# First layer's mixing with tokens on partitions: split weights everywhere, and the 31-tap convolution as a 128-point Fourier transform

## The chip, the cores and the metric

The kernel runs on one core of a Trainium2 chip. The metric is device time in microseconds (us) of the whole program, median of the timed runs. One further execution was profiled; all rows below are from that one. Engine names are those of the profile: PE is TensorE, PEld its weight load, DVE is VectorE, ACT is ScalarE, POOL is GpSimd, SP is SyncE, whose queue issues nearly all transfers.

## The reference, cut to what matters

A decoder trunk of two layers, 256 tokens, width 1024, all in float32. Each layer is a half-step SwiGLU network, a mixing part and a second half-step network. The mixing part of the first layer, the one that is changed, is this:

```python
hn = rms_norm(h, mix_norm_g[0])
u = hn @ a_w_in[0]                                  # 1024 x (768 + 768 + 256)
a, gate, q_mem = u[..., :768], u[..., 768:1536], u[..., 1536:]
c = a * sigmoid(gate)
c = depthwise_causal_conv(c, taps=31) + dw_bias     # 768 channels
primary = silu(layer_norm(c, ln_g, ln_b))
mem_out = memory_attention(q_mem, rms_norm(mem), w_mem_kv[0], ...)   # 4 heads of 64, 256 memory rows
h = h + concatenate([primary, mem_out]) @ w_o[0]    # 1024 x 1024
```

The second layer's mixing part has attention over a shared key and value set in place of the convolution; its keys and values from the memory (`w_mem_kv[1]`) do not depend on the tokens, and the kernel makes them during the first layer's mixing part.

## The kernel before, in words

Weights stream from main memory in chunks of 128 x 2048 floats (1 MB) through three buffers `raw`. A chunk is used in one of two ways.

- Split: each half of 1024 columns is turned by ACT into `wh`, the part that one pass of PE takes (type fp32r), and by DVE into the rest, `wl = raw - wh` (`half_hi`, `half_chunk`, lines 199 to 226). There are four buffers of each. A product is then three one-pass terms: `wh` by the high part of the input, `wh` by its low part, `wl` by the high part (`mm3`, `mm3_tok`). In the networks the first two terms are one instruction of 512 columns (`mm2`).
- Whole: `raw` goes to PE as float32 (`raw_chunk`). PE then runs two instructions for each product.

The program is a chain of stages with PE working through nearly all of it: network `a` (names `ag`, `au`, `ao`), the first mixing part, network `b`, the shared keys and values (`kv`), network `c`, the second mixing part, network `d`.

The first mixing part (lines 801 to 1044) works with channels on partitions. `glu_in` makes the six 128-channel blocks of value (`ca`) and gate (`cg`), 256 token columns at a time; blocks 0 and 1 from split weights, blocks 2 to 5 from whole ones, and so is the query product `mq`. `conv` then adds the 31 taps of blocks 0 to 4 one tap at a time: `DVE_TAPS` of them as a multiply-add on DVE (line 892), `POOL_TAPS` as a product on ACT (line 883) and an addition on POOL (line 884). Block 5 goes to PE as 32 products with diagonal matrices `diag`, which ACT builds during the down projection of network `a` (line 798). The layer norm sums over channels with two sets of products (`lnm`, `lnv`). Meanwhile PE makes the memory keys and values of the next layer from whole weights (`mkv`), runs the attention of two pairs of heads (`am00`, `am01`) and opens the output projection (`oao`) with the attention's 256 rows, again from whole weights. The 768 rows of the convolution follow from split weights. The order around these steps is partly written by hand with `go`, partly left to the scheduler.

The second mixing part is built from named steps whose order on PE, DVE, ACT and POOL is one written list, `MIX1`; all its weights are split. The engines take their steps strictly in this order.

Of the kernel before, what the change touches and what calls it, by code (L numbers as in the profile page):

```python
# [32 lines left out]
PAD = TAPS - 1  # L33
# [10 lines left out]
SPLIT_CHUNKS = 2  # L44

DVE_TAPS = (14, 31, 0, 31, 18)
POOL_TAPS = (17, 0, 31, 0, 13)

HALF_CH = P // 2
SHIFTS = (TAPS + 1) // 2  # L50
PADH = PAD // 2
MEM_AT = 9
FIRST_CAT = 3

# [21 lines left out]
Q_AT = 6  # L76
CNR_AT = 4

# [15 lines left out]
V_TAP = 72  # L94
V_CB = V_TAP + CC * TAPS
V_LG = V_CB + CC
V_LB = V_LG + CC
V_PP = V_LB + CC
V_PB = V_PP + 4 * SHIFTS

V_QG = V_PB + 2
NV = V_QG + 2

G_MQ, G_MK, G_K, G_Q = 0, 1, 3, 4
NG = 5
# [4 lines left out]

@with_exitstack
def tile_kernel(ctx: ExitStack, tc: tile.TileContext, w, xT, memT, pos, vec, hg, const, out):
# [25 lines left out]
    nc.scalar.dma_start(vt[:, :V_TAP], vec[:, :V_TAP])  # L138
# [8 lines left out]
    onel = cp.tile([P, 1], F32, name="onel")  # L147
    nc.vector.memset(onel, 1.0 / PW)
    onem = cp.tile([P, P], F32, name="onem")
    nc.vector.memset(onem, 1.0 / PW)  # L150
# [18 lines left out]

    def tables(func):  # L170

        behind(nc.scalar.activation(warm, onec, func), state["func"])
# [20 lines left out]

    def raw_chunk():
        assert state["half"] == 0
        state["chunk"] += 1
        return load_chunk(state["chunk"] - 1)
# [84 lines left out]
    def y_both(name):  # L282
        whole = yp.tile([P, KD, 2, SEQ], F32, name=name + "w", tag="y")
        return y_tiles(name), whole[:, :, 0]

    def scaled_split(y, src, k, g, on_dve=False):

        if isinstance(y, tuple):
            y, yw = y
            if on_dve:  # L290
                nc.vector.tensor_scalar(yw[:, k], src, vt[:, g + k:g + k + 1], None, op0=ALU.mult)
                nc.scalar.activation(y[:, k, 0], src, AF.Copy, scale=vt[:, g + k:g + k + 1])
            else:
                nc.scalar.activation(yw[:, k], src, AF.Copy, scale=vt[:, g + k:g + k + 1])
                nc.scalar.activation(y[:, k, 0], yw[:, k], AF.Copy)
            nc.vector.tensor_tensor(y[:, k, 1], yw[:, k], y[:, k, 0].bitcast(F32), op=ALU.subtract)
            return
# [50 lines left out]
    def ffn(name, y, acc, nexts, store=False, both=False, hook=None, after=None, hook_down=None, r=None, plan=None):  # L348
# [98 lines left out]
        ys = [(y_both if both else y_tiles)(f"{name}y{i}") for i in range(len(nexts))]  # L447
        acc = new_acc(name + "acc")
        it = tiles_of(KD * KF // 8)
        for m in range(KD):  # L450
# [21 lines left out]
            last = both and m == KD - 1  # L472
            if last:
                square_sum(f"{name}q{m}", acc, x[:, m], False, nc.vector)
            for yy, g in zip(ys, nexts):
                state["ends"] = scaled_split(yy, x[:, m], m, g, last)
            if not last:
                square_sum(f"{name}q{m}", acc, x[:, m], m == 0)
# [35 lines left out]
    def proj(name, y, *uses):  # L514
# [3 lines left out]
        if isinstance(y, tuple):  # L518
            raw = raw_chunk()
            for k in range(KD):  # L520
                for t in range(NT):
                    mmul(os_[t][:, :n], y[1][:, k, t * P:(t + 1) * P], raw[:, k * n:(k + 1) * n],
                         start=k == 0, stop=k == KD - 1)
        else:
            per = HC // n
            for k0 in range(0, KD, per):
                wh, wl = half_chunk()
                for t in range(NT):
                    for i in range(per):
                        k = k0 + i  # L530
                        mm3_tok(os_[t][:, :n], wh, wl, y, t, k, slice(i * n, (i + 1) * n), k == 0, k == KD - 1)
# [35 lines left out]
    def queries(name, e, g, dst, pair0, defer):  # L567


        def use(t, o):  # L570
            ms = heads_norm(f"{name}s{t}", o, 4)
            qg = tp.tile([P, MW], F32, name=f"{name}t{t}", tag="tok")
            q3 = qg.rearrange("p (h d) -> p h d", d=HD)
            nc.vector.tensor_tensor(q3, o.rearrange("p (h d) -> p h d", d=HD), gain_b(g, 4), op=ALU.mult)
            v = tp.tile([P, 4], F32, name=f"{name}v{t}", tag="hv")
            nc.vector.tensor_scalar(v, ms, e[:, t:t + 1], None, op0=ALU.add)
            c = tp.tile([P, 4], F32, name=f"{name}c{t}", tag="hr")
            nc.gpsimd.tensor_tensor(c, v, mhalf[:, :4], op=ALU.pow)
            nc.vector.tensor_tensor(q3, q3, c[:, :, None].to_broadcast([P, 4, HD]), op=ALU.mult)
            def turn():  # L580
                to_heads_T(f"{name}p{t}", qg, dst, pair0, t, "sc")
            defer.append(turn)
        return use

    def attend_pair(name, qT, kT, v, vcol0, pair, causal, tag, done, o_tag=("mm", 4)):

        hs = [slice(e * HD, (e + 1) * HD) for e in range(2)]
        S = [psum(f"{name}s{e}", *(("mm", 4) if tag == "mm" else ("sc", 2))) for e in range(2)]
        spans = ((0, P), (P, 3 * P)) if causal else ((0, SEQ), (SEQ, 2 * SEQ))
        width = spans[1][1]  # L590
        opened = []
        for t, (lo, hi) in enumerate(spans):
            for e in range(2):

                i = mmul(S[e][:, lo:hi], qT[hs[e], pair, t * P:(t + 1) * P], kT[hs[e], pair, :hi - lo],
                         start=t == 0 or not causal, stop=not causal, skip_group_check=causal)
                if t:
                    behind(i, opened[e])
                opened.append(i)
        if causal:  # L600
            for e in range(2):

                mmul(S[e].rearrange("p (a b) -> p a b", b=2 * P)[:, :, :P], identb,
                     maskb[:, None, :].to_broadcast([P, 2, P]), start=False, stop=True, skip_group_check=True)
        yield

        nb = [tp.tile([P, NT], F32, name=f"{name}n{e}", tag="nb", bufs=4) for e in range(2)]
        for e in range(2):
            if causal:
                for t, (lo, hi) in enumerate(spans):  # L610
                    in_order("V", nc.vector.tensor_reduce(nb[e][:, t:t + 1], S[e][:, lo:hi], axis=AX.X, op=ALU.min))
            else:
                in_order("V", nc.vector.tensor_reduce(nb[e], S[e].rearrange("p (t k) -> p t k", t=NT), axis=AX.X,
# [57 lines left out]
    def go(head, n):  # L671
        for _ in range(n):
            next(head)
# [830 lines left out]
```

## Time and profile before

| | us |
|---|---|
| median of three timed runs (979.95 to 980.14) | 980.0 |
| span of the profiled execution, first to last instruction | 978.8 |
| PE busy | 971.9 |
| PEld busy | 848.1 |
| DVE busy | 727.8 |
| ACT busy | 592.4 |
| POOL busy | 132.4 |

Busy time of PE counts each matmul from its start to its modelled end, and successive matmuls overlap in it; what a matmul costs in a stream is the distance from one start to the next. The median lies 1.2 us above the span; that part lies outside the first and the last instruction. The granted clock of PE is 1.000 on average.

### The profile page before, as it was taken

To read this page: it belongs to the slowest core of one execution; us is meant where nothing else is said; L and a number is where in the kernel's file an instruction comes from. 1 tells how busy PE (TensorE), PEld (TensorE's weight loads), DVE (VectorE), ACT (ScalarE), POOL (GpSimd) and SP (SyncE) were. 2 spreads that over 40 slices of the span, in tenths; PEclk is the share of its full clock that TensorE was granted. 3 is DMA by queue.
4 is the path that set the end of the run, shared out by engine and by line. 5 is a ranking of instruction groups with operands and counts; after the bars stand their busy time and mean duration, and the time that the engine had idled before them with its cause. 6 is when DMAs were issued, how large, how long until landed. Compare 5 with 4: busy or idle time off the path is not lost.

```text
span 978.8 us, 15511 instructions
## 1 busy us (share of the span) xinstructions
PE 971.9 (99%) x5793; PEld 848.1 (87%) x5793; DVE 727.8 (74%) x1305; ACT 592.4 (61%) x1150; POOL 132.4 (14%) x154
## 2 busy tenths in 40 slices
PE   9999999999999999999999999999999999999998
PEld 6888888898779888888888888888897898888887
DVE  7888776679967777777766877776669578777663
ACT  6675577747667655555556655565547666555542
POOL 0121000128812000000122100000133130000000
PEclk9999999999999999999999999999999999999999
DMA  8655555533325555555555555455552255555550
GB/s 324 246 180 177 209 173 181 207 130 130 106 110 175 213 177 199 184 175 202 183 178 176 206 178 204 179 191 197 175 172 85 92 174 209 178 209 173 191 217 22
DMA packets 26427, 173.44 MB, mean 177 GB/s; under 512 B 3184, under 2 KB 4848, under 8 KB 6000
## 3 DMA queue, kind: packets, MB, share of 16 engines
q1 hardware_dynamic: 26064, 172.28, 50.9%
q8 instruction: 45, 0.74, 0.3%
q14 instruction: 30, 0.25, 0.1%
q10 hardware_dynamic: 288, 0.17, 0.1%
HBM read 171.39 MB, written 1.05 MB: 176 GB/s over the span
## 4 chain that ended last, share of the span: by engine, by line
PE 92%; DVE 4%; POOL 2%; ACT 1%; issue 1%; POOLq 0%
PE cg L175 7%; PE bg L175 6%; PE bu L175 6%; PE do L175 6%; PE co L175 6%; PE bo L175 6%; PE ao L175 6%; PE ag L175 6%; PE au L175 6%; PE dg L175 6%; PE cu L175 6%; PE du L175 6%; PE kv L175 3%; PE oao L175 2%; PE obo L175 2%; PE mkv L175 2%
## 5 line engine op out<-in xcount | busy, mean ns | idle before, releaser
L211 ACT ACTIVATE wh<-raw 128x1024 fp32r<-128x1024 f32 (+1 forms) x310 | 325.0, 1050 | 312.1 <-PE bg L175 27.5
L215 DVE TENSOR_TENSOR wl<-raw,wh 128x1024 fp32r<-128x1024 f32 (+1 forms) x310 | 376.9, 1218 | 178.6 <-ACT wh L211 177.7
L175 PE MATMUL ag<-y,wh 128*128 128x512 f32 x176 | 63.7, 397 | 0.0
L175 PE MATMUL bg<-oay,wh 128*128 128x512 f32 x176 | 63.5, 399 | 0.0
L175 PE MATMUL bu<-oay,wh 128*128 128x512 f32 x176 | 63.4, 398 | 0.0
L175 PE MATMUL au<-y,wh 128*128 128x512 f32 x176 | 63.1, 394 | 0.0
L175 PE MATMUL dg<-oby,wh 128*128 128x512 f32 x176 | 62.5, 392 | 0.0
L175 PE MATMUL cg<-by,wh 128*128 128x512 f32 x176 | 62.3, 392 | 0.0
L175 PE MATMUL du<-oby,wh 128*128 128x512 f32 x176 | 62.3, 391 | 0.0
L175 PE MATMUL cu<-by,wh 128*128 128x512 f32 x176 | 62.2, 392 | 0.0
L175 PE MATMUL co<-chs,wh 128*128 128x512 f32 (+1 forms) x198 | 61.9, 369 | 0.0
L175 PE MATMUL do<-dhs,wh 128*128 128x512 f32 (+1 forms) x198 | 61.9, 369 | 0.0
L175 PE MATMUL bo<-bhs,wh 128*128 128x512 f32 (+1 forms) x198 | 61.9, 369 | 0.0
L175 PE MATMUL ao<-ahs,wh 128*128 128x512 f32 (+1 forms) x198 | 61.9, 368 | 0.0
L175 PE MATMUL co<-chs,wl 128*128 128x256 f32 x176 | 49.7, 283 | 0.0
L175 PE MATMUL do<-dhs,wl 128*128 128x256 f32 x176 | 49.7, 283 | 0.0
L175 PE MATMUL bo<-bhs,wl 128*128 128x256 f32 x176 | 49.6, 283 | 0.0
L175 PE MATMUL ao<-ahs,wl 128*128 128x256 f32 x176 | 49.6, 283 | 0.0
L175 PE MATMUL bg<-oay,wl 128*128 128x256 f32 x176 | 49.5, 281 | 0.0
L175 PE MATMUL cg<-by,wl 128*128 128x256 f32 x176 | 49.5, 281 | 0.0
L175 PE MATMUL bu<-oay,wl 128*128 128x256 f32 x176 | 49.4, 281 | 0.0
L175 PE MATMUL dg<-oby,wl 128*128 128x256 f32 x176 | 49.4, 280 | 0.0
(947 smaller groups left out, 2430.0 us busy)
## 6 DMA issues: line engine op xcount, KB each, us to landing
raw<-in_w SPq DMA_DIRECT2D x158, 1024.0 KB, 4.8
raw<-in_w SPq DMA_DIRECT2D x5, 512.0 KB, 8.8
mT<-in_memT SPq DMA_DIRECT2D x1, 1024.0 KB, 7.4
out<-x SPq DMA_DIRECT2D x8, 128.0 KB, 1.7
raw<-in_w SPq DMA_DIRECT2D x2, 256.0 KB, 4.2
x<-in_xT SPq DMA_DIRECT2D x1, 512.0 KB, 7.3
x<-in_xT SPq DMA_DIRECT2D x2, 128.0 KB, 3.1
x<-in_xT SPq DMA_DIRECT2D x1, 256.0 KB, 5.3
```

What stands on the lines that cost most here:

```text
L175: return in_order("P", nc.tensor.matmul(*a, **k))
L211: state["act"] = nc.scalar.activation(wh[:, s], raw[:, s], AF.Copy)
L215: state["dve"] = nc.vector.tensor_tensor(wl[:, s], raw[:, s], wh[:, s].bitcast(F32), op=ALU.subtract)
```

## The change

All of the first mixing part is rewritten with tokens on partitions, as named steps in one written order, `MIX0`, like that of the second. The second part's functions `heads_pair`, `room_of` and `stepper` are now shared by both; its own order does not change.

- Every weight of the stage is split: value and gate, query, memory keys and values of the next layer, all eight row blocks of the output projection. That is 26 halves of 1024 columns where the stage had 10.
- Value and gate come in three groups (A, B, C) of 256 channels: inputs are the stationary operand, and 512 weight columns (256 value, 256 gate) stream.
- The convolution of a group is: three blocks of 128 rows (tokens 0 to 127, tokens 128 to 255, and a third one put together from the first 32 tokens of both halves, the last 32 of the first half and 32 rows of zeros), a forward transform by one 128 x 128 matrix (`F`), a product with the taps' spectrum (`z`, `y`), an inverse transform (`I`). Transforms are whole float32 products. The first 32 outputs of each half are taken from the third block (`e1`).
- The spectrum `spec` is made once during network `a` from a small table (`spectra`).
- The layer norm uses the statistics instructions of DVE (`b`, `L.a`), then the result is transposed back to channels on partitions (`L.T`).
- The query's gain moves into the memory key's (`gq`, index 2).

Four constants are loaded next to the memory input, and the conv taps leave the vector table. The memory input's scaled copy for the next layer (`next_mem`) is now made, split, in the down projection of network `a`, where the diagonals were built.

```diff
-        if isinstance(y, tuple):
-            raw = raw_chunk()
-            for k in range(KD):
-                for t in range(NT):
-                    mmul(os_[t][:, :n], y[1][:, k, t * P:(t + 1) * P], raw[:, k * n:(k + 1) * n], ...)
...
-def conv(c):
...
-            for i in range(nd + 1, nd + np_):
-                nc.scalar.activation(q, win(c, i), AF.Copy, scale=tap[c][i])
-                state["pool"] = nc.gpsimd.tensor_tensor(cv[:, c], cv[:, c], q, op=ALU.add)
...
-            for i in range(1, nd):
-                nc.vector.scalar_tensor_tensor(cv[:, c] if end else o, win(c, i), tap[c][i], o, ...)
...
+            nc.sync.dma_start(spec[:, S_F:S_G + P], wave[:, :2 * P])
+            nc.sync.dma_start(roots, wave[:3 * REACH, 2 * P:])
+            nc.sync.dma_start(tapw, taps)
+            nc.sync.dma_start(spec[:, S_BIAS:S_BIAS + PW], bias)
...
+    def spectra():
+        nc.scalar.activation(rootr, roots, AF.Copy)
+        nc.scalar.activation(tapr, tapw, AF.Copy)
+        nc.vector.tensor_tensor(tapr[low], tapw[low], tapr[low].bitcast(F32), op=ALU.subtract)
+        for i in range(3):
+            for at in range(512 * i, 512 * (i + 1), MW):
+                mmul(o[:, at % 512:at % 512 + MW], rootr[:, ...], tapr[:, c:c + MW], start=True, stop=True)
+            nc.scalar.activation(spec[:, 512 * i:512 * (i + 1)], o, AF.Copy)
...
+    def project(name, yy, first, ks, n):
+        per = HC // n
+        for k in ks:
+            wh, wl = halves[first + k // per][:2]
+            for t in range(NT):
+                mm3_tok(pss[name][t][:, :n], wh, wl, yy, t, k, slice(k % per * n, (k % per + 1) * n), ...)
...
+    def gated_group(name, g, first):
...
+            @step(f"{name}.s{t}")
+                state["func"] = A(nc.scalar.activation(sg[t], pss[name][t][:, MW:], AF.Sigmoid, scale=rc[:, t:t + 1]))
+            @step(f"{name}.h{t}")
+                V(nc.vector.scalar_tensor_tensor(h3[:, t, gs], pss[name][t][:, :MW], rc[:, t:t + 1], sg[t], ...))
+            @step(f"{name}.k{i}")
+                V(nc.vector.tensor_copy(h3[to * REACH:(to + 1) * REACH, 2, gs], h3[fr * REACH:(fr + 1) * REACH, t, gs]))
...
+            @step(f"{name}.F{b}")
+                mmul(out_of("X", b, n), spec[:, S_F:S_F + P], h3[:, bs, gs], start=True, stop=True)
+            @step(f"{name}.z{b}")
+                V(nc.vector.tensor_tensor(z1[:, bs], X, wide(S_A, whole, n), op=ALU.mult))
+                V(nc.vector.tensor_tensor(z2[high, bs], X[low], wide(S_B, low, n), op=ALU.mult))
+                V(nc.vector.tensor_tensor(z2[low, bs], X[high], wide(S_B, high, n), op=ALU.mult))
+            @step(f"{name}.y{b}")
+                G(nc.gpsimd.tensor_tensor(z1[:, bs], z1[:, bs], z2[:, bs], op=ALU.add))
+            @step(f"{name}.I{b}")
+                mmul(out_of("O", b, n), spec[:, S_G:S_G + P], z1[:, bs], start=True, stop=True)
+        @step(f"{name}.e02")
+            V(nc.vector.tensor_tensor(cv[:, :, gs], out_of("O", "02", 2), wide(S_BIAS, whole, 2), op=ALU.add))
+        @step(f"{name}.e1")
+            for t, fr in ((0, 2), (1, 0)):
+                V(nc.vector.tensor_tensor(cv[:REACH, t, gs], pss[name + "O1"][r, :MW], spec[r, S_BIAS + ...], op=ALU.add))
+            @step(f"{name}.b{t}")
+                V(nc.vector.bn_stats(bn[:, t, g], cv[:, t, gs]))
...
+    @step("L.a")
+            V(nc.vector.bn_aggr(agg[:, t], bn[:, t].rearrange("p g s -> p (g s)")))
+        V(nc.vector.tensor_scalar(var, agg[:, :, 1], EPS, None, op0=ALU.add))
+    @step("L.r")
+        G(nc.gpsimd.tensor_tensor(rl, var, mhalf[:, :NT], op=ALU.pow))
+    @step(f"L.z{t}")
+            V(nc.vector.tensor_scalar(cv[:, t], cv[:, t], agg[:, t, 0:1], rl[:, t:t + 1], ...))
+    @step(f"L.T{i}")
+            for c in range(2 * i, 2 * i + 2):
+                for t in range(NT):
+                    transp(pss["L", i][:, ...], cv[:, t, c * P:(c + 1) * P], ident)
...
+MIX0 = """
+hi0 hi1 lo0 hi2 A.0 zero lo1 hi3 lo2 hi4 A.1 lo3 lo4 A.2 hi5 lo5 A.3a hi6 B.0 lo6 cn hi7 A.3b cv ce cr lo7 B.1 hi8
...
+B.F1 hi12 A.F02 B.z1 C.0 A.z02 B.y1 A.F1 hi13 lo12 Q.1 A.y02 A.z1 lo13 A.y1 A.I02 q.s hi14 C.1 q.r A.e02 q.p lo14
...
+B.I02 C.h1 M.0 n0.mn1 n0.ex0 C.k1 C.k0 C.k2 B.e02 n0.ex1 n0.nm0 C.F02 B.e1 hi17 n0.tr0 n0.nm1 M.1 n0.ev0 C.z02 hi18
+n1.S lo17 hi19 C.y02 C.F1 n1.mn1 n0.tr1 M.2 C.z1 n1.ex1 n1.mn0 C.y1 n0.ev1 n1.ex0 n1.nm1 C.I02 B.b0 C.I1 xs C.e02
+M.3 C.e1 hi20 n1.nm0 C.b1 B.b1 n0.o hi21 C.b0 L.a n1.tr1 n0.hi lo18 n1.tr0 L.r K.t1 n1.ev0 n1.ev1 K.t0 L.z0 K.s1
+n1.o K.s0 L.z1 K.v1 n0.lo n1.hi L.T0 lo19 K.v0 L.T1 c0.s L.T2 o.6 c0.h n1.lo c1.s lo20 c1.h c2.s c0.l c2.h lo21 c3.s
...
```

Steps with `02` work on the first two blocks together, 512 columns; those with `1` on the third, 256. `L.z` takes 768 columns, `L.T0` to `L.T2` are twelve transposes. In `MIX0`, `hi` and `lo` are the two splits of a half, `Q` the query product, `M` and `K` the next layer's memory keys and values, `n0` and `n1` the two pairs of heads (`S` scores, `mn` minimum, `ex` exponential, `nm` division, `tr` transposes, `ev` their eviction, `o` the product with the values), `c` the norm's gain, silu and split per channel block, `o.k` the output rows of block k.

## Rows read from the trace of the kernel before

**Rows 1.** The head of the page: span, then busy time, share of the span and number of instructions of each engine.
```profile
span 978.8 us, 15511 instructions
PE 971.9 (99%) x5793; PEld 848.1 (87%) x5793; DVE 727.8 (74%) x1305; ACT 592.4 (61%) x1150; POOL 132.4 (14%) x154
```
**Rows 2.** Busy time by stretch: start and end, length, then PE, PEld, DVE, ACT, POOL busy (with instruction counts), granted clock, DMA share, GB/s. The stretches are all that lies before the first mixing part, the first mixing part, the second mixing part.
```profile
0.00:205.70 205.70, 204.22 (x1163) 176.16 (x1164) 156.66 (x281) 142.44 (x300) 19.80 (x23) 1.00 0.61 211
205.50:312.20 106.70, 105.29 (x633) 90.15 (x632) 87.46 (x199) 71.06 (x156) 51.98 (x70) 1.00 0.36 123
717.70:790.80 73.10, 72.61 (x599) 63.85 (x598) 54.47 (x141) 49.51 (x130) 25.10 (x26) 1.00 0.31 105
```
**Rows 3.** The chain that ended last, in order of time, in the first mixing part: start, length, engine, tile, line, count.
```profile
212.08 2.87 PE ca L175 x24
...
217.82 3.46 PE ca L175 x16
...
235.92 3.14 DVE cvp L892 x8
...
254.97 1.42 POOL hc L884 x2
...
267.73 1.19 PE am00s L175 x6
...
270.00 1.91 PE mkv L175 x4
271.91 2.59 PE lnm L175 x12
274.50 3.43 PE mkv L175 x8
277.94 0.87 PE am00pp L178 x8
...
280.53 2.68 PE lnv L175 x24
283.21 1.01 PE am00o L175 x8
...
297.01 0.22 PE mk1p L178 x2
...
312.18 0.35 PE bu L175 x2
```
**Rows 4.** Groups of PE instructions in the first mixing part: line, engine, operation, output and inputs, shape, count, then busy time, mean ns of one, idle time before them.
```profile
L175 PE MATMUL mkv<-raw,hc 128*128 128x512 f32 x32 | 14.5, 596 | 0.0
L175 PE MATMUL ca<-ay0w,raw 128*128 128x256 f32 x64 | 14.5, 379 | 0.0
L175 PE MATMUL cg<-ay0w,raw 128*128 128x256 f32 x64 | 14.5, 379 | 0.0
...
L175 PE MATMUL oao<-hc,raw 128*128 128x256 f32 x32 | 7.3, 382 | 0.5 <-ACT hc L668 0.5
L175 PE MATMUL cvp<-hc,diag 128*128 128x128 f32 x64 | 7.3, 275 | 0.0
L175 PE MATMUL mq<-raw,ay0w 128*128 128x256 f32 x32 | 7.1, 379 | 0.0
...
L175 PE MATMUL ca<-ay,wh 128*128 128x256 f32 x32 | 5.9, 285 | 0.0
...
L175 PE MATMUL am00s<-mk,q0T 64*128 64x256 f32 x8 | 1.4, 402 | 0.9 <-ACT q0T L511 0.9
```
**Rows 5.** The chain again, during network `a`: the memory keys and values of the first layer, split weights, 512 columns streaming.
```profile
60.18 10.92 PE mkv L175 x48
```
**Rows 6.** Groups of instructions of DVE and POOL over the whole span, shapes kept apart, columns as in rows 4.
```profile
L215 DVE TENSOR_TENSOR wl<-raw,wh 128x1024 fp32r<-128x1024 f32 x302 | 371.7, 1232 | 177.0 <-ACT wh L211 176.1
L892 DVE SCALAR_TENSOR_TENSOR cvp<-hc,vt,cvp 128x256 f32<-128x256 f32 x88 | 40.6, 484 | 1.5
...
L303 DVE SCALAR_TENSOR_TENSOR cy<-x,vt,cy 128x256 fp32r<-128x256 f32 x8 | 6.7, 843 | 0.6 <-ACT cy L302 0.6
L215 DVE TENSOR_TENSOR wl<-raw,wh 128x512 fp32r<-128x512 f32 x8 | 5.2, 688 | 1.6 <-ACT wh L211 1.6
...
L1240 DVE TENSOR_SCALAR room<-room 128x256 f32<-128x256 f32 x14 | 4.7, 364 | 0.1
...
L303 DVE SCALAR_TENSOR_TENSOR y<-x,vt,y 128x256 fp32r<-128x256 f32 x8 | 3.5, 480 | 0.0
...
L884 POOL TENSOR_TENSOR hc<-hc,cq 128x256 f32<-128x256 f32 x58 | 42.5, 735 | 12.6 <-ACT cq L883 8.8 <-POOL hc L884 0.2
```
**Rows 7.** PE in order of time in the second mixing part: scores, transposes and value products of masked pairs of heads.
```profile
756.99 0.93 PE L175 MATMUL a4s<-kvs,q1T 64*128 64x128 f32 x8
...
758.18 0.88 PE L178 MATMUL a2pp<-cst,room 128*128 128x128 f32 x6
759.00 0.87 PE L175 MATMUL a1o<-room,kvs 128*64 128x256 f32 x8
759.80 0.93 PE L175 MATMUL a5s<-kvs,q1T 64*128 64x128 f32 x8
```
**Rows 8.** The chain in the second mixing part where it runs through DVE: one split.
```profile
741.58 1.13 DVE wl L215
```
**Rows 9.** Busy time by stretch, as in rows 2, at the time when the four constants would land.
```profile
30.00:38.00 8.00, 8.00 (x49) 7.00 (x48) 7.93 (x17) 6.30 (x14) 0.00 (x0) 1.00 0.59 217
```

More of the change, by code (lines that the diff above doesn't have):

```diff
@@ L446, in ffn @@
             tables(after)
-        ys = [(y_both if both else y_tiles)(f"{name}y{i}") for i in range(len(nexts))]
+        ys = [y_tiles(f"{name}y{i}") for i in range(len(nexts))]
         acc = new_acc(name + "acc")
@@ L585, in attend_pair, with room_of, place @@
[L585 removed]
+    def room_of(tile_):
+        taken = [0]
+        def place(*shape):
+            n = int(np.prod(shape))
+            taken[0] += n
+            assert taken[0] <= tile_.shape[1], taken
+            piece = tile_[:, taken[0] - n:taken[0]]
+            if len(shape) == 1:
+                return piece
+            names = [f"d{i}" for i in range(len(shape))]
+            return piece.rearrange(f"p ({' '.join(names)}) -> p {' '.join(names)}", **dict(zip(names, shape)))
+        return place
@@ L587, in attend_pair, with stepper, step, add @@
+    def stepper():
+        steps = {}
+        def step(name):
+            def add(f):
+                assert name not in steps, name
+                steps[name] = f
+            return add
+        return steps, step
+    def heads_pair(step, place, pr, pTs, cat, name, qT, kT, v, pair, causal, kc, s_tag, o_tag):
         hs = [slice(e * HD, (e + 1) * HD) for e in range(2)]
-        S = [psum(f"{name}s{e}", *(("mm", 4) if tag == "mm" else ("sc", 2))) for e in range(2)]
+        vc = [slice(pair * P + e * HD, pair * P + (e + 1) * HD) for e in range(2)]
@@ L600, in attend_pair @@
-        if causal:
-            for e in range(2):
[L603 to L613, printed above, removed]
-                                                      op=ALU.min))
@@ new lines, in tile_kernel, with next_mem @@
+    my1 = []
+    def next_mem(m):
+        if m == 0:
+            my1.append(y_tiles("my1"))
+        scaled_split(my1[0], mT[:, m], m, V_MEM + KD)
+    (y,), acc = ffn("a", y, None, (V_MIX,), hook=prepare, after=AF.Sigmoid, hook_down=next_mem,
+                    plan={(2, "u", 1): "mean", (3, "g", 3): "rows"})
+    place = room_of(cp.tile([P, KF * 2 * SEQ], F32, name="hc", tag="hs"))
+    steps, step = stepper()
+    flat = place(3 * PW)
+    h3 = flat.rearrange("p (b c) -> p b c", b=3)
+    zs = [[place(3, MW) for _ in range(2)] for _ in range(2)]
@@ L1031, in tile_kernel, with cat, _ @@
-    for k, (wh, wl, *_) in enumerate(halves):
+    halves, pss, late = {}, {}, {}
+    def cat():
+        if "cat" not in late:
+            late["cat"] = y_tiles("cat0")
+        return late["cat"]
+    for i in range(HEAD1):
+        @step(f"hi{i}")
+        def _(i=i):
+            halves[i] = half_hi()
+            for s in halves[i][2]:
+                j = A(halves[i][3](s))
+            if i == HEAD0 + 1:
+                behind(j, state["ends"][0])
+        @step(f"lo{i}")
+        def _(i=i):
+            for s in halves[i][2]:
+                j = V(halves[i][4](s))
+            if i == HEAD0:
+                behind(j, state["ends"][1])
@@ L1032, in tile_kernel, with rows @@
+    def rows(i, k):
+        wh, wl = halves[i][:2]
+        if "o" not in late:
+            *_, late["o"] = out_sums("oa")
         for m in range(KD):
             s = slice(m * P, (m + 1) * P)
-            mm3(o[m], (wh[:, s], wl[:, s]), cat, k, False, False, skip_group_check=True)
-        if k < NT:
-            mem_turns[k]()
+            opens = k == CC
+            j = mm3(late["o"][m], (wh[:, s], wl[:, s]), cat(), k, opens and m % 2 == 0, False, skip_group_check=True)
+            if opens:
+                out_first(j, m)
@@ L1037, in tile_kernel @@
+    for i, k in enumerate((CC, CC + 1, 0, 1, 2)):
+        step(f"o.{k}")(lambda i=i, k=k: rows(18 + i, k))
+    state["order"] = "PVAG"
+    for name in MIX0:
+        steps[name]()
     state["order"] = ""
+    o, cat = late["o"], late["cat"]
     ys = y_tiles("oay")
```

846 lines of the change are left out of this document (364 added, 482 removed).

## Prediction, written before the changed kernel was run

> **What bounds the kernel now.** I read the head of the page first: PE is busy for 971.9 of 978.8 us [rows 1]. Overlapping matmuls make that figure useless as a measure of slack, so the next view is the stretches: the stage that changes takes 106.7 us, and in it DVE has 87.5, ACT 71.1 and POOL 52.0 us of work beside a PE that is never idle for long [rows 2]. The third view is the chain in order of time. It enters the stage on PE (`ca`), goes over to DVE's taps (`cvp`) and POOL's additions (`hc`) and comes back to PE at 267.7 with the scores [rows 3], where PE has waited 0.9 us for the transposed query [rows 4]. So two things of almost the same length run side by side: PE's instructions, and the taps on three engines. A shorter PE stream alone would only wait longer at 267.7. The change takes the taps away as well, so what PE issues after it, plus its waits, is the time of the stage, provided that DVE, which gets new work, stays shorter.
>
> **Prices on PE**, from start to start in a stream. One-pass products: 256 columns 2.87/24 = 0.120 us, 512 columns 10.92/48 = 0.2275 [rows 3, 5]. Whole float32, each instruction, two to a product: 256 columns 3.46/16 = 0.216, 512 columns 3.43/8 = 0.429, 128 columns 2.68/24 = 0.112 [rows 3]. A transpose: 0.22/2 = 0.11 [rows 3].
>
> **What PE does now in the stage.** Value and gate, blocks 0 and 1: 4 x 24 products, 11.5 us; blocks 2 to 5: 128 instructions, 27.7. Query: 32, 6.9. Memory keys and values: 32 of 512 columns, 13.7. Diagonals: 64 of 128 columns, 7.2. Norm: 2.6 and 2.7, and four broadcasts of rows, 0.4. Attention's rows of the output: 32, 6.9 [rows 3, 4]. Together 79.6. What stays: scores 2.3 (267.7 to 270.0), transposes of probabilities 2 x 0.87, value products 2 x 1.01, eight transposes of query and key 0.9, the mean 0.3, six blocks of output rows 144 x 0.12 = 17.3 [rows 3]: 24.5. Sum 104.1; the stage has 106.7, so 2.6 us are waits (the first products of the next stage included).
>
> **What it does after.**
> - Value and gate: 3 groups x 8 row blocks x 2 token halves x 3 terms = 144 products of 512 columns, 32.8 us for 39.2. Three one-pass terms cost less than one whole product, and streaming 512 columns costs less per column than 256.
> - Query: 48 of 256 columns, 5.8 for 6.9. Memory: 48 of 512, 10.9 for 13.7. Attention's output rows: 48 of 256, 5.8 for 6.9.
> - Transforms: per group one product of 512 and one of 256 columns in each direction, whole: 12 x 0.429 + 12 x 0.216 = 7.7, for the diagonals' 7.2.
> - Norm: twelve transposes, 1.3, for 5.7 of sums and broadcasts.
>
> This is 64.3 for 79.6, with the unchanged part 88.8 us. The spectrum adds six products of 256 columns, 0.7 us, in network `a`. PE's net: 15.3 - 0.7 = 14.6 us less.
>
> The Trainium skill ("TensorE: Matmul & The Clock Gate", Back-to-back issue gap) gives N/2.4 + 2.5 ns for a warm matmul, 216 ns at 512 columns; this trace has 227.5 [rows 5], with a weight load before every product. By that rule the 192 products of 512 columns would take 2.3 us less, and the forecast would be 964.5.
>
> **Does DVE stay shorter?** Splits: 26 x 1.23 = 32.0 us. A group: two gatings 0.97, three copies and two short additions at 0.42 each 2.1, the spectrum product on 512 columns 3 x 0.69, on 256 columns 3 x 0.42, the bias 0.69, two statistics 0.84; 7.9 us, three groups 23.8. Attention 8.5 and query 1.7, the operations of now; norm 0.7 and two passes over 768 columns at 0.95; keys 2.1, splits of the rows 2.5, ends of the output 8.6. Sum 82 us. The prices are those of rows of the same width [rows 6]: 512 columns 0.688, 256 columns 0.36 to 0.48, and 768 extrapolated from 0.364 by 256 columns per 0.27. No row shows a statistics instruction, a copy of 32 partitions or an access across partitions; below they can cost 0.36, above 0.84, the slowest row of that width; I take 0.42, since the unshared rows of the width lie at 0.36 to 0.48. The upper end adds at most 24 x 0.4 = 10 us to DVE. A mean holds overlap with the next instruction: the same split takes 1.23 as a mean and 1.13 in a chain [rows 8], so 133 instructions at 0.085 less make 71. DVE is at 71 to 82 of 89 us: shorter than PE, but at places not by much. POOL gets three groups at 2.2, some seven small powers and gains at about 1 and the seven sums of squares it has now, some 21 us for 52 [rows 2]. An addition of 512 columns on POOL lies between 0.735 [rows 6] and twice that; I take 1.47, and it is covered by a whole group's stream.
>
> **Waits after.** The tight stretch is from the end of group C's products to the norm's first transpose, `L.T0`. By the written order PE has in it both sets of scores 2.3, the inverse transforms of B 1.3, the memory product 10.9, both transforms of C 2.6, sixteen transposes 1.8 and the value products 2.0: 20.9 us. DVE has C's gatings 0.97, copies 1.26, spectrum products 3.3, bias and short additions 1.5, statistics 1.3; what is left of B 1.95; the softmax of both pairs 7.7 (four minima of 512 columns, four divisions of 0.88 with two passes at 0.364 in each, two evictions); two splits 2.5; the norm's sums 0.7 and its two passes 1.9; and in between POOL's power, 1.0: 24.0 us, or 21.6 with some 29 overlaps of 0.085. DVE also starts about 1 us late, since it sits in a split when C's products end. So PE waits 1.7 to 4.1 us there; late with `L.T0` are `o.0` and every row product behind it. The last part alone, behind C's inverse transform, is 8.0 us on DVE and POOL beside 5.6 on PE. As a check, the second mixing part already runs a written order with split weights. Its PE work is 384 products at 0.12, two unmasked pairs 6.0, six masked ones at 2.81 (756.99 to 759.80 [rows 7]), sixteen transposes and a mean 2.1: 71.1 of its 73.1 us [rows 2], waits 2.0, with DVE at 75%. I take 4.0 us for the new stage: the upper end of the tight stretch, since DVE is fuller here. No waits and 9 us are the ends.
>
> **At no cost.** The four constants (0.9 MB, less 0.1 MB of taps) go out on SP's queue ahead of the next weight chunk; at 217 GB/s [rows 9] they hold it up by 3.7 us. The cover: the memory input, 1 MB, goes out at the same place already, and after it PE is busy for 8.00 of 8.00 us with the transfer engines at 0.59 [rows 9]. Without the cover: 970.5. In network `a`, ACT loses the 64 diagonals and gets 8 scalings and five steps of the spectrum, DVE gets 8 subtractions; PE covers them (ACT 142 of 206 us busy, DVE 157 [rows 2]). In the stage ACT gives up 58 tap products and gets 16 splits more; it had 71 of 107 us [rows 2]. The query's gain moves into an eviction that exists already.
>
> **Sum.** PE 14.6 us less, waits 4.0 for 2.6: 13.2 less. On the median, 1.2 above the span: 980.0 - 13.2 = **966.8 us**.
>
> **Rivals.**
> 1. *DVE becomes the bound.* For it: at 82 us plus 10 of unknowns it passes PE, and a busy POOL stretches it: the same multiply-add of 256 columns takes 0.843 at `cy` and 0.480 at `y` [rows 6]. Against it: POOL falls from 52 to 21 us. If every POOL operation ahead of the norm (13 us) stopped DVE for its length, DVE would have 95 us, the stage 95 + 4, and the time 980.0 - 106.7 + 99 + 0.7 = 973. The Trainium skill ("SBUF — State Buffer", Who interferes with whom) has this as a rule: a DVE instruction with two SBUF inputs and a GpSimd instruction that reads SBUF exclude each other, the later one waiting for the whole of the other. The pair `cy` and `y` is of the size of such a wait. Chance 0.15.
> 2. *No waits at all*, the written order covering the norm: 962.8. Against it the 8.0 beside 5.6 at the norm. Chance 0.10, with what lies a little above.
> 3. *DVE's instructions stretch beside POOL, and the kernel gets slower.* Place: the tight stretch. The gain of 13.2 is used up when DVE's 24 us there become 37, that is at 1.55 times their rows; `cy` over `y` is 1.76, and at that ratio the stretch takes 18 us more: 985. Against it: that ratio was met beside POOL additions, and POOL has some 3.5 us in this stretch. Chance 0.04.
> 4. *The constants come late*, 970.5. Chance 0.04.
>
> The forecast itself, waits of 2 to 7 us, has 0.67 and by itself 964.8 to 969.8. The range of 962.5 to 973 leaves out the rest of rivals 1 and 3. What a measurement can tell from no change is about 0.2%, 2 us: faster 0.95, same 0.01, slower 0.04.
>
> **What would show it.** Right: products of 512 columns 0.2275 apart, transforms 0.43 per instruction at 512 columns, a stage of some 93 us, the chain on PE except around `L.T0`, where PE waits for DVE (`L.z1`). Wrong: the chain on DVE through groups B and C with splits well above 1.23 (rivals 1, 3); weight loads that wait for a split or a transfer; statistics or short copies far over 0.42; a granted clock below 1.00 in the stage, which no row before shows.

## The result, and the profile after

The changed kernel takes 965.58 us (median of four runs, 964.69 to 966.17), the kernel before 980.07 beside it: ratio 0.9851, 95% interval 0.9837 to 0.9865. The forecast was 966.8. The profiled execution took 966.11 us, its span is 964.3.

The head of the page after, answering [rows 1]:

```profile
span 964.3 us, 15067 instructions
PE 956.6 (99%) x5699; PEld 832.9 (86%) x5699; DVE 718.7 (75%) x1243; ACT 562.5 (58%) x1026; POOL 103.3 (11%) x101
```

Busy time by stretch, columns as in [rows 2]: all ahead of the changed stage, the stage, the rest.

```profile
0.00:206.70 206.70, 204.00 (x1167) 175.96 (x1168) 162.43 (x286) 132.27 (x241) 19.81 (x23) 1.00 0.60 213
206.70:297.80 91.10, 90.35 (x533) 76.18 (x533) 72.77 (x131) 51.17 (x89) 22.89 (x17) 1.00 0.41 144
297.80:964.30 666.50, 662.25 (x4002) 580.74 (x4001) 483.46 (x827) 379.02 (x697) 60.57 (x61) 1.00 0.50 176
```

The stage went from 106.7 us [rows 2] to 91.1, 15.6 less. The rest is 666.5 for 666.6 (312.2 to 978.8 before). Ahead of the stage this one execution took 1.2 us more; the profiles below show that this arises in the first 25 us and belongs to the execution, not to the change. DVE has 72.8 us of work beside 91, POOL 22.9 for 52, and the clock is 1.00 throughout.

The chain that ended last, in order of time, answering [rows 3]:

```profile
206.93 9.57 PE A L182 x42
...
229.24 2.87 PE Q L182 x24
232.11 0.43 PE BX L182 x2
232.54 0.86 PE AX L182 x2
233.40 2.76 PE C L182 x12
...
251.40 1.49 PE BO L182 x4
252.89 2.77 PE M L182 x12
...
268.66 1.01 PE n0o L182 x8
269.67 1.04 PE n1pp L185 x8
...
270.80 0.61 ACT hc L647
...
271.44 1.08 PE n1o L182 x8
272.53 1.46 PE lt L185 x12
273.99 11.51 PE oao L182 x96
...
297.80 0.35 PE bu L182 x2
```

The taps (`cvp`) and POOL's additions have left the chain. It is PE from end to end but for one step: at 270.7 PE waits for ACT to empty the transposed probabilities of memory pair 1 (`hc` L647). The list of waits (who waited for whom, total, times, longest) has that wait, and it is PE's only one in the stage; DVE in turn waits most, in total, for ACT's first half of a split:

```profile
DVE wl L217 <- ACT wh L213: 7.4, 8, 1.5
...
PE n1o L182 <- ACT hc L647: 0.7, 1, 0.7
```

The groups of DVE and POOL in the stage, columns as in [rows 6], where the forecast had only neighbours to go by:

```profile
L217 DVE TENSOR_TENSOR wl<-raw,wh 128x1024 fp32r<-128x1024 f32 x25 | 30.4, 1220 | 7.7 <-ACT wh L213 7.4
...
L907 DVE COPY hc<-hc 32x256 f32<-32x256 f32 x9 | 2.6, 285 | 0.2
...
L952 DVE BATCH_NORM_STATS2 hc<-hc 128x6 f32<-128x256 f32 x6 | 2.2, 410 | 0.0
...
L1081 DVE TENSOR_SCALAR hc<-hc 128x768 f32<-128x768 f32 x2 | 1.3, 676 | 0.0
...
L1076 POOL TENSOR_TENSOR hc<-hc,mhalf 128x2 f32<-128x2 f32 x1 | 1.6, 1614 | 5.9 <-DVE hc L1072 5.9
...
L931 POOL TENSOR_TENSOR hc<-hc 128x512 f32<-128x512 f32 x3 | 6.9, 2301 | 15.4 <-DVE hc L927 15.4
L931 POOL TENSOR_TENSOR hc<-hc 128x256 f32<-128x256 f32 x3 | 3.2, 1083 | 15.2 <-DVE hc L927 15.2
```

### The profile page after: what moved, and what is told of

The parts are those of the page before. It is cut to its first block, busy times and chain, and to the rows that moved or that the text cites. A ratio compares the mean times of both kernels' runs of the same rounds, so it can differ in the third digit from the quotient of the medians.

```text
span 964.3 us, 15067 instructions
## 1 busy us (share of the span) xinstructions
PE 956.6 (99%) x5699; PEld 832.9 (86%) x5699; DVE 718.7 (75%) x1243; ACT 562.5 (58%) x1026; POOL 103.3 (11%) x101
## 4 chain that ended last, share of the span: by engine, by line
PE 94%; DVE 3%; DMA 1%; ACT 1%; POOL 0%; SPq 0%; issue 0%; ACTq 0%
PE dg L182 6%; PE bg L182 6%; PE du L182 6%; PE bu L182 6%; PE do L182 6%; PE co L182 6%; PE ao L182 6%; PE cg L182 6%; PE bo L182 6%; PE cu L182 6%; PE ag L182 6%; PE au L182 6%; PE kv L182 3%; PE obo L182 2%; PE oao L182 2%; PE A L182 1%
## 5 line engine op out<-in xcount | busy, mean ns | idle before, releaser
L213 ACT ACTIVATE wh<-raw 128x1024 fp32r<-128x1024 f32 (+1 forms) x326 | 341.7, 1050 | 344.4 <-PE dg L182 28.1
L217 DVE TENSOR_TENSOR wl<-raw,wh 128x1024 fp32r<-128x1024 f32 (+1 forms) x326 | 396.4, 1217 | 183.0 <-ACT wh L213 181.7
L182 PE MATMUL ao<-ahs,wh 128*128 128x512 f32 (+1 forms) x198 | 61.1, 367 | 0.0
L182 PE MATMUL co<-chs,wh 128*128 128x512 f32 (+1 forms) x198 | 61.1, 367 | 0.0
L182 PE MATMUL do<-dhs,wh 128*128 128x512 f32 (+1 forms) x198 | 61.1, 367 | 0.0
L182 PE MATMUL bo<-bhs,wh 128*128 128x512 f32 (+1 forms) x198 | 61.1, 367 | 0.0
L182 PE MATMUL du<-oby,wl 128*128 128x256 f32 x176 | 49.4, 281 | 0.0
L182 PE MATMUL cu<-by,wl 128*128 128x256 f32 x176 | 49.3, 280 | 0.0
L182 PE MATMUL ag<-y,wl 128*128 128x256 f32 x176 | 49.1, 281 | 0.1
L182 PE MATMUL au<-y,wl 128*128 128x256 f32 x176 | 49.1, 281 | 0.0
```

The lines of the kernel that those rows point to most:

```text
L182: return in_order("P", nc.tensor.matmul(*a, **k))
L213: state["act"] = nc.scalar.activation(wh[:, s], raw[:, s], AF.Copy)
L217: state["dve"] = nc.vector.tensor_tensor(wl[:, s], raw[:, s], wh[:, s].bitcast(F32), op=ALU.subtract)
```

## The experiments

Names beginning with b_ are edits of the kernel before, with a_ of the changed one. A stage is measured in one profile from the first product of `A` (206.93 in the chain above) to the first of `bu` (297.80): 90.87 us in the changed kernel. It tells tenths of a microsecond apart, where the medians of two kernels do not.

### Which of the two sides set the stage before: stream or taps

Three edits of the kernel before. b_split6 turns all six blocks of value and gate into split weights; b_fewtaps cuts the taps that go one at a time to two per block.

```diff
-SPLIT_CHUNKS = 2                     # b_split6 and b_fewtaps_split6
+SPLIT_CHUNKS = 6
-DVE_TAPS = (14, 31, 0, 31, 18)       # b_fewtaps and b_fewtaps_split6
-POOL_TAPS = (17, 0, 31, 0, 13)
+DVE_TAPS = (2, 2, 0, 2, 2)
+POOL_TAPS = (0, 0, 2, 0, 0)
```

> The kernel before with 2 taps instead of 31 for channel blocks 0 to 4 (the output is not the reference's: 29 taps of five blocks are left out); PE's instructions stay the same. Theory (PE's stream sets the stage, the taps run beside it and cost only PE's waits of about 2.6 us): 1 to 2.5 us faster, 977.5 to 979. Rival (the gain of the change comes from the taps that leave DVE, ACT and POOL): 10 us or more faster, below 970.

> The kernel before with value and gate of blocks 2 to 5 from split weights too (192 products of 0.12 for 128 instructions of 0.216: PE 4.6 us less; DVE 8 splits of 1.23 = 9.8 us more, ACT 8.5 us more); taps and all else stay. Theory (the taps' chain is as long as PE's stream, so less PE work alone only waits, and the splits lengthen the taps' chain): 2 to 9 us slower, 982 to 989. Rival (PE's sum alone sets the time): 4.6 us faster, 975.5.

> Both edits together (2 taps for blocks 0 to 4, the other 29 left out, so the output is not the reference's; split weights for all of value and gate). Theory: with the taps gone PE's 4.6 us show, on top of what few taps alone give: 5 to 7 us faster than before, 973 to 975. Rival (DVE is the bound): no faster than with few taps alone.

Measured beside 980.35: b_fewtaps 979.78 (ratio 0.9996, 0.9987 to 1.0006), no difference that can be measured, where 1 to 2.5 us were expected; b_split6 988.85 (1.0085, 1.0069 to 1.01), 8.5 us slower; both together 975.35 (0.9947, 0.9932 to 0.9962), 5.0 us faster. The chain of b_fewtaps shows why taps alone bring next to nothing: it no longer touches DVE's taps, and PE's instructions fill nearly the same time. The stage, from the first product of `ca` to the first of `bu`, is 105.82 us for 106.51 before. PE's wait for the query at 267.7 falls from 0.9 us to 0.3, and that is nearly all that the taps had cost it.

```profile
238.05 3.45 PE ca L175 x16
241.50 3.45 PE cg L175 x16
```

With the split as well, each of those blocks is 24 one-pass products, 2.88 for 3.45 us, as the forecast has it, and the stage is 101.24 us, 4.6 less than with few taps alone:

```profile
234.64 2.88 PE ca L175 x24
237.52 2.88 PE cg L175 x24
```

Split weights without fewer taps put eight more splits on DVE and ACT, which the taps already fill. PE's waits in b_split6, and two pairs of neighbouring stretches (columns as above):

```profile
PE cg L175 <- ACT cq L883: 5.4, 1, 5.4
PE am00s L175 <- ACT q0T L511: 3.2, 1, 3.2
```

```profile
236.00:240.00 4.00, 0.96 (x4) 0.99 (x5) 3.90 (x10) 2.76 (x7) 3.66 (x5) 0.85 0.08 33
240.00:244.00 4.00, 4.00 (x28) 4.00 (x26) 3.89 (x11) 3.11 (x9) 3.40 (x6) 0.72 0.00 0
...
272.00:276.00 4.00, 2.15 (x10) 2.15 (x12) 3.72 (x9) 1.67 (x4) 2.21 (x4) 0.62 0.56 233
276.00:280.00 4.00, 4.00 (x12) 2.24 (x10) 3.75 (x8) 0.00 (x0) 0.00 (x0) 0.53 0.00 0
```

PE stands still for most of 236 to 240 and is busy throughout the next four microseconds, in which the granted clock is 0.72. From 272 it is busy for 2.15 of four at a clock of 0.62, and in the next four the clock is 0.53 though PE is busy throughout; that is close to the lower level of 1.2 GHz (0.50). Eight products `am01s` took 1.71 us there and 1.02 in b_fewtaps. So a PE that waits pays twice: the stage is 115.58 us, 9.1 longer than before; PE's listed waits are 10.5 us for 1.4 and its products 4.6 less, which leaves, as an estimate, 4.6 us to the lowered clock. In these edits neither half gains by itself and together they do, as the prediction's first part says. They stand in for the halves of the change only in part: b_fewtaps leaves taps out instead of computing them otherwise, and b_split6 splits four blocks and not the whole stage.

### What PE issues sets the stage now

a_cols256 gives back the wide streams, a_wholeM gives the memory product `M` whole weights again.

```diff
-                mm3_tok(pss[name][t][:, :n], wh, wl, yy, t, k, ...)
+                for b in range(0, n, MW):                       # a_cols256
+                    for l, r in ((0, wh), (0, wl), (1, wh)):
+                        mmul(pss[name][t][:, b:b + MW], yy[:, k, l, s], r[:, at + b:at + b + MW], ...)
```

```diff
-        step(f"M.{i}")(lambda i=i: project("M", my1[0], 14, (2 * i, 2 * i + 1), 2 * MW))
+        step(f"M.{i}")(lambda i=i: memory((2 * i, 2 * i + 1)))  # a_wholeM: one float32 product each, from raw
-hi14 lo14 hi15 lo15 hi16 lo16 hi17 lo17                         # steps of the written order
+rw0 rw1                                                         # two whole chunks are loaded
```

> The changed kernel, with each product of 512 streamed columns in the four projections A, B, C and M (value and gate, memory keys and values) issued as two of 256 columns: 384 instructions in the place of 192. Same results, same splits, same order of the steps. Theory (what PE issues sets the stage): 384 x 0.120 - 192 x 0.2275 = 2.4 us more, so about 968.0 against 965.6. Rival (DVE or the chain of the transform sets the stage, or the width of a stream costs nothing): below 966.3.

> The changed kernel with one part undone: the product of the memory keys and values of the second layer (M) takes whole float32 weights, as before. PE gets 32 instructions of 0.429 for 48 of 0.2275, 13.7 for 10.9 us, 2.8 more; DVE loses four splits of 1.23 in the stage (two of them between group C's products and the norm) and eight subtractions in network a, ACT loses four splits. Theory (PE's stream sets the time): 2.1 to 2.8 us more (PE's wait of 0.7 ahead of n1o can be filled), 967.7 to 968.4. Rival (DVE sets the stretch before the norm, so that two splits less are worth more than PE's 2.8): 965.6 or less.

Measured beside 980.22: a_cols256 966.84, a_wholeM 967.30. Their stages are 92.87 us (205.07 to 297.94), 2.0 more than 90.87, and 93.56 (205.53 to 299.09), 2.7 more. Both are near what PE's instructions alone say (2.4 and 2.8), though the medians lie a little under the times expected. Beside the 964.95 of a_dve_early (below), whose stage is as long as the changed kernel's and which was timed with them, they are 1.9 and 2.4 us longer. a_wholeM's DVE had 4.3 us of work less in its stage (68.5 for 72.8) without any use for it. PE's stream is the bound; the wide streams are worth 2.0 us, a little under the forecast, because a product of 512 columns took 0.227 to 0.228 in A and B (9.57/42 in A) but some 0.2305 in C and M (2.76 or 2.77 for 12).

### Where DVE has no room

The forecast put a tight stretch between the end of C's products and `L.T0`. Two additions of 512 columns, whose result nobody uses, go into that stretch in a_dve_tight and to a place in group A where DVE idles in a_dve_early.

```diff
+    def extra():
+        for t in range(2):
+            V(nc.vector.tensor_tensor(sq0..., spec[:, :512], spec[:, 512:1024], op=ALU.add))
+    step("dd")(extra)
-... n0.o hi21 C.b0 L.a n1.tr1 ...       # a_dve_tight
+... n0.o hi21 C.b0 dd L.a n1.tr1 ...
-... hi7 A.3b cv ce ...                  # a_dve_early
+... hi7 A.3b dd cv ce ...
```

> The changed kernel with two additions of 512 columns on DVE whose result nobody uses, 2 x 0.69 = 1.38 us, put into the written order right ahead of L.a, so between the end of group C's products and the norm's transposes. Theory (DVE and PE arrive at L.T0 together: the last norm pass ends at 272.41, PE begins the transposes at 272.46): 1.2 to 1.4 us more, so about 966.9. Rival (PE alone sets this stretch, DVE has room): 965.6.

> The control of the same two additions of 512 columns on DVE, 1.38 us, put instead ahead of cv, in group A, where DVE is idle for 2.05 us before the mean. Theory (DVE has room everywhere but in the stretch before the norm): no change, 965.6. Rival (DVE's total work sets the stage): 1.4 us more, 967.0, here as well as in the stretch before the norm.

Measured: a_dve_tight 966.27, a_dve_early 964.95. Stages 91.97 (205.29 to 297.26) and 90.87 (205.46 to 296.33): 1.1 us more for two additions that take 1.31 us in the chain of the tight stretch, and nothing for the same work elsewhere. The chain of a_dve_tight now runs over DVE from C's inverse transform to the value product `n1o`:

```profile
262.96 0.87 PE CO L182 x2
...
267.21 0.60 DVE hc L1125
267.83 0.69 DVE hc L1125
...
268.97 1.13 DVE wl L217
270.10 0.61 DVE hc L649
270.75 1.08 PE n1o L182 x6
```

Line 1125 is the added work. Line 649 is DVE's half of the eviction `n1.ev` of pair 1's transposes; in the changed kernel ACT's half (`hc` L647) lets `n1o` go, here DVE's does. The norm's transposes behind it take 1.61 us for 1.46; the second norm pass ends at 271.96, when they have begun already (271.76). So DVE and PE arrive together there, and DVE's margin in that stretch is some 0.2 us (1.31 - 1.10).

The same profiles settle the 1.2 us ahead of the stage. All these kernels are the same up to `A`, and it begins at 206.93 in the changed kernel's profile but at 205.07 in a_cols256 and 205.46 in a_dve_early. The difference is there before 25 us have passed: the first products of network `a`'s norm (`anrp`) start at 24.64 and 23.17, and from them to `A` it is 182.29 us in both, for 182.28 in the kernel before (23.39 to 205.67). What differs ahead of that is when the last 512 KB of the input land (issues by line, size, median us from issue to landing; the changed kernel, then a_dve_early):

```profile
x<-in_xT SPq DMA_DIRECT2D x1, 512.0 KB, 9.3
```

```profile
x<-in_xT SPq DMA_DIRECT2D x1, 512.0 KB, 7.3
```

That these landings are the whole difference is not shown: a_fill has `anrp` at 23.61 with 7.4 us.

### Using the wait that is left

a_fill moves ACT's emptying of the memory accumulators forward and lets PE do the output rows of memory pair 0 while ACT and DVE empty pair 1's transposes.

```diff
-... B.b1 n0.o hi21 C.b0 L.a n1.tr1 n0.hi lo18 n1.tr0 L.r K.t1 n1.ev0 n1.ev1 K.t0 L.z0 K.s1
-n1.o K.s0 L.z1 K.v1 n0.lo n1.hi L.T0 lo19 K.v0 L.T1 c0.s L.T2 o.6 c0.h n1.lo ...
+... B.b1 n0.o K.t1 K.v1 C.b0 L.a n1.tr1 K.t0 K.v0 lo18 n1.tr0 L.r n0.hi n0.lo n1.ev0 n1.ev1
+L.z0 o.6 hi21 K.s1 L.z1 n1.o K.s0 n1.hi L.T0 lo19 L.T1 c0.s L.T2 c0.h n1.lo ...
```

> The changed kernel with the written order altered around the one wait of PE in the stage (0.7 us ahead of n1o, for ACT's eviction n1.ev0): ACT empties the memory product's two accumulators (K.t, K.v) right after it, and PE does the output rows of memory pair 0 (o.6, 24 products of 256 columns, 2.9 us) between the transposes n1.tr0 and the product n1.o. The same instructions, another order. Theory (what is left to gain in the stage is PE's wait): the stage is 0.4 to 0.7 us shorter (90.9 us from the first product of A to the first of bu now), about 965.0 in all, which only the stretches of the profile can tell from no change. Rival (DVE's chain to L.z1 sets this stretch anyway and PE waits at L.T0 instead): the stage is 90.9 or longer.

Measured: 965.31 beside 980.27 (0.9848, 0.9833 to 0.9863); the stage 90.56 (205.90 to 296.46), 0.3 less where 0.4 to 0.7 were expected. The wait of 0.7 is gone, but PE is now held for about 0.3 us ahead of the row products, whose input comes from `n0.lo`:

```profile
269.54 0.43 DVE cat L669
270.02 3.02 PE oao L182 x23
273.04 1.01 PE n1o L182 x8
```

### Streams of the same form at two speeds

Comparing the profiles showed something that no step of the prediction has. The down projections of all four networks, which the change does not touch, are faster after, and gate and up of network `d` slower. Groups over the whole span, the kernel before, then the changed one:

```profile
L175 PE MATMUL dg<-oby,wh 128*128 128x512 f32 x176 | 62.5, 392 | 0.0
...
L175 PE MATMUL do<-dhs,wh 128*128 128x512 f32 (+1 forms) x198 | 61.9, 369 | 0.0
```

```profile
L182 PE MATMUL dg<-oby,wh 128*128 128x512 f32 x176 | 63.5, 399 | 0.0
...
L182 PE MATMUL do<-dhs,wh 128*128 128x512 f32 (+1 forms) x198 | 61.1, 367 | 0.0
```

In the chain this is 2.77 or 2.83 us for 16 products of gate or up (2.83 in `b` before, in `b` and `d` after), and some 61 or 62 us for a down projection. Behind the stage the two nearly cancel: three times 0.8 less, 2.0 more. The fourth 0.8, in network `a`, makes up for the spectrum's 0.7. The tiles lie elsewhere in SBUF in the changed kernel: `hs` at 58048 bytes instead of 56032, `wh` at 138016 instead of 131936. Three kernels move every tile by the same distance with an unused one in front:

```diff
+    pad = cp.tile([P, 8], F32, name="pad")        # b_pad32; 24 in b_pad96, 520 in a_pad2080
```

> The kernel before with one unused tile of 32 bytes a partition, which moves the networks' hidden tile from an address of 32 modulo 64 bytes to 0 modulo 64, as in the changed kernel, and the inputs and split weights from 32 to 0. Theory (the four down projections are 0.73 us shorter each in the changed kernel because of where the hidden tile lies): down projections of 61.15 us for 61.9, 3 us less from them. Rival (something else in the change sets it): 61.9 as before, 980.

> The kernel before with an unused tile of 96 bytes on each partition ahead of the others: hs lies at 56128 instead of 56032, at 64 within 128 bytes as in the changed kernel (58048). No instruction changes but one small fill. If the place of hs within 128 bytes sets the rate of the down projections: 61.15 us each instead of 61.9, 3.0 us less in all, 977.1. If not: 980.1.

> The changed kernel with an unused tile of 2080 bytes on each partition ahead of the others, so that hs lies at 60128 instead of 58048, the same place within 4096 bytes as the 56032 of the kernel before, and every tile behind it lies 2080 bytes further. No instruction changes but one small fill. The down projections of all four networks took 61.9 us before and 61.15 after. If the place of hs within 4096 bytes sets their rate: 61.9 each, 3.0 us more in all, 968.6. If the place does not matter (rival: the sequence of the work does): 61.15, 965.6.

Measured: b_pad32 980.73 (1.0004, 0.9994 to 1.0013), b_pad96 981.58 (1.0011, 1.0001 to 1.002), a_pad2080 965.34. The down projections did not move in any of them (61.9, 61.9, 61.1): the place of `hs` by itself does not set their speed. Only b_pad96 shows another speed: gate and up of network `a` became slower, 64.3 for 63.7 and 63.7 for 63.1. The chain there has both speeds within the one network, from the same tiles, with the memory's keys and values in between:

```profile
53.95 2.77 PE ag L177 x16
...
88.19 2.83 PE ag L177 x16
```

So where the tiles lie does not decide alone. Network `c` does the same in the kernel before: 2.82 or 2.83 in its first blocks, 2.77 in the others. What these three leave untouched is the distance between the tile that streams and the tile that is loaded as weights. `hs` and `wh` lie at the same place within 64 bytes before (32 and 32) and not after (0 and 32), while `y` and `wh` do so in both. a_fill_y32 puts 32 bytes ahead of `y` alone.

```diff
+    pad = yp.tile([P, 8], F32, name="pad", tag="pad", bufs=1)
```

> The kernel of a_fill with an unused tile of 32 bytes on each partition ahead of the two buffers of the networks' input y, so that y lies at 0 within 64 bytes while the split weights wh and wl lie at 32, as hs (0) and wh (32) already do in the changed kernel; before and in b_pad96 hs and wh lay at the same place within 64 bytes, and the down projections took 61.9 us instead of 61.15. Theory (a product runs slower where the streamed tile and the loaded weights lie at the same place within 64 bytes): the down projections stay at 61.15, and gate and up of b and d fall from 2.83 to 2.77 us or less per 16 products (44 times each 16 in a network), some 5 us less in all, about 960. Rival (the place of the streamed tile against the weights does not set the rate): gate and up keep 2.83 in b and d, 965.3.

Measured beside 980.65: **960.61** (959.86 to 960.98; ratio 0.9794, 0.9781 to 0.9807), 4.7 us under a_fill. Gate and up of `b` and `d` are at 2.77, and the down projections stay:

```profile
L185 PE MATMUL dg<-oby,wh 128*128 128x512 f32 x176 | 62.4, 391 | 0.0
...
L185 PE MATMUL do<-dhs,wh 128*128 128x512 f32 (+1 forms) x198 | 61.1, 367 | 0.0
```

The run came out as that theory said, and it is the fastest kernel here. Behind the stage its profile is 662.2 us long for 666.5 in a_fill's. It is not the whole rule. In the projections of the stage, where `y` is loaded and `wh` streams, the same 32 bytes made products slower (42 products of A in 9.80 us for 9.57). In the output rows, where the buffer of `y` streams, they made them faster (87 in 10.15 for 10.44). The buffers of the norms behind `y` moved as well. And gate and up of `a` and `c` ran at 2.77 for the most part with `y` and `wh` at the same place, so that place alone doesn't make a stream slow. Moving `y` and what lies behind it changed the speed; for `hs` it is an inference from which kernels moved it. Why `b` and `d` were the slow ones stays open, and so does a rival that no run tests: that a stream takes up one of two speeds when it starts, by the timing of what runs beside it, and keeps it until it is interrupted, as network `a` of b_pad96 would have it. The 32 bytes would then have changed that timing.

## Why the prediction was right, point by point

- **The bound.** Right: stream and taps were two things of almost the same length. Taking one alone gave nothing or made it slower, both together 5.0 us less. The 2.6 us called waits were not what the taps cost: PE's list of waits before has 1.4, and only 0.6 of them went with the taps (b_fewtaps). The rest of the 2.6 is no wait in that list.
- **PE's terms.** Right. Forecast 64.3 for 79.6 us in the stage, 15.3 less; the stage is 15.6 us shorter, and what it holds beyond the forecast products is about equal (2.3 us for 2.6). The transforms took 0.43 an instruction (`AX` 0.86 for two of 512 columns), products of 512 columns 0.227 to 0.231, the twelve transposes of the norm 1.46 for 1.3. The spectrum cost 0.7 us in network `a` as forecast: two entries of the chain there, 0.48 and 0.24.
- **The gap of 216 ns.** The Trainium skill ("TensorE: Matmul & The Clock Gate", Back-to-back issue gap) would have made the 192 wide products 2.3 us shorter. The trace disagrees by 11 to 15 ns a product, with a weight load ahead of each; the price read from a row held. That section of the Trainium skill gives the 216 ns for a single, isolated product, and 131 ns at 512 columns for a stream of weight loads and products; no stream here comes near the latter.
- **DVE.** Right at the lower end: 72.8 us, forecast 71 to 82. A copy of 32 partitions took 0.285 (taken as 0.42), a norm pass over 768 columns 0.68 (0.95), a statistics instruction 0.41 (0.42). Rivals 1 and 3 needed DVE to stretch beside POOL, and it did so only here and there: at 280.23 one product of 256 columns took 0.96 us while POOL had begun one of 0.74 just ahead of it. That pair fits the rule of the Trainium skill ("SBUF — State Buffer", Who interferes with whom), by which the later of two such instructions waits. Its twin at 279.25 took 0.42 although POOL was in a small power since 278.4, so the rule is not visible in each pair. POOL has too few instructions left (22.9 us, forecast some 21) for this to set the time.
- **POOL's additions.** Mis-sized: an addition of 512 columns was put between 0.735 us and twice that and taken as 1.47; the three took 2.30 as a mean. Each began just behind a split of DVE (at 236.12, 246.15 and 259.12 for splits at 236.08, 246.10 and 259.00). The one of 256 columns that did so, at 238.71, took 1.77, the other two 0.74. So here it was POOL that was held, and not DVE. It cost the stage nothing, since PE had other groups to stream.
- **The waits: the mis-sized term.** I took 4.0 us, the upper end of the tight stretch; the stage holds 91.1 - 88.8 = 2.3 us beyond PE's forecast work. Of that, 0.7 is the one wait; the transforms (8.1 us for 7.7), the wide products (44.1 for 43.7) and the first products of the next stage make most of the rest. The place was right: DVE and PE arrive together at `L.T0` (last norm pass done at 272.41, transposes begun at 272.46), and a_dve_tight shows that there is no room. The size was not. From the end of C's products to `L.T0` the columns of [rows 2] read:

```profile
250.34:272.46 22.12, 21.37 (x109) 15.05 (x109) 19.92 (x47) 15.20 (x34) 4.60 (x3) 1.00 0.18 66
```

DVE is busy for 19.9 us, below the 21.6 to 24.0 that I summed, because the norm passes, copies and divisions were cheaper than their neighbours' rows; PE has 21.4 for 20.9. Behind C's inverse transform DVE took 6.9 us (265.50 to 272.41) for the 8.0 of the forecast. PE's wait fell on ACT's eviction just ahead, not on `L.z1`. The median lies 1.2 us under the forecast. In the profile, where the span is 14.5 us shorter for the 13.2 forecast, this term makes 1.7 less, the part behind the stage 0.1 less, and the part ahead of it 0.5 more (1.2 for the spectrum's 0.7).
- **Constants at no cost.** Right: the way from `anrp` to the stage, in which they land, takes 182.29 us in the changed kernel and 182.28 before, with 0.7 more for the spectrum and 0.8 less for the down projection in it. The stage begins at 205.07 to 206.93 us in the profiles of the changed kernel and its edits, and at 205.18 (b_fewtaps) to 206.69 (b_pad96) in those of the kernel before and its edits.
- **Not foreseen.** Unchanged streams ran at other speeds (above). Behind the stage this made 2.4 us less and 2.0 more and so hardly touched the sum; ahead of it, 0.8 less, which a late input hid in the profile. By luck, not by argument: no term of the forecast covered it.

## What to carry to other kernels

When two engines set a stage side by side, price the change for both sides and test the halves: the half that shortens the longer-looking side can gain nothing, and the other half can lose. Where work is gathered into the last stretch ahead of a join, sum each engine over that stretch alone; totals of the stage (DVE 73 of 91 us) hide that its margin there is 0.2 us. If PE is the bound, compare the time of identical product streams across stages and across two builds; a difference of 2% between them is worth more than a reordering was here (4.7 us for 0.3), and a few bytes of padding may buy it. No rule for the padding came out: of four that were tried one gave 4.7 us, two did nothing, and one cost about 1.

## What the runs showed of the hardware that was not expected

- The same stream of products takes 2.77 or 2.83 us per 16 at a granted clock of 1.00. Moving the streamed tile (and the buffers behind it) 32 bytes against the weights changed it in two networks and took 4.7 us off the kernel. The place does not decide alone: in b_pad96 one network ran at both speeds from the same tiles. The Trainium skill ("TensorE: Matmul & The Clock Gate", Step-by-step: what each phase is for) says that loading the next weights does not take read bandwidth from the running matmul, over ports of their own; that gives no reason for a speed that changes with where the streamed tile lies, and no run here shows the mechanism.
- In b_split6 PE stood for 5.4 and for 3.2 us. In the stretches of four microseconds in which it started again the granted clock was 0.85 and 0.62, and in the next four 0.72 and 0.53, though PE was then busy throughout. The changed kernel has no such stretch.
- The very small powers on POOL (two columns) took 1.6 us in the tight stretch, begun at 269.49 just behind a split of DVE (269.32), and 0.7 in group A; the forecast had 1.0. Additions on POOL show the same: 1.77 us for 0.74 where they begin behind a split.
